# Four edits in a two-layer trunk: other delays, a later constant load, a new planner cost, and six batches whose first product waits for ScalarE

## The chip, the cores and the metric

The kernel runs on one NeuronCore of a Trainium2 chip; the other cores are idle. TensorE (PE in the rows, its weight loads PEld) multiplies, VectorE (DVE) and ScalarE (ACT) do the elementwise work, GpSimd (POOL) almost nothing, and SyncE's queue (SP) issues nearly all transfers. The metric is device time in microseconds (us) of one execution.

## The reference, cut to what matters

Sequence 512, width 1024, float32. Layer 0 has a gated short convolution and a gated linear recurrence (HGRN2) side by side; layer 1 has stick-breaking attention with 16 heads of width 64. Each layer ends with a squared-ReLU MLP of width 4096, and the six modulation vectors of a layer come from one product with `c`.

```python
for layer in range(2):
    mod = silu(c) @ ada_w[layer] + ada_b[layer]
    shift1, scale1, gate1, shift2, scale2, gate2 = split(mod, 6)
    h = rms_norm(x, norm_mix[layer]) * (1 + scale1) + shift1
    y = mixer_conv_hgrn(h, ...) if layer == 0 else mixer_stick_breaking(h, ...)
    x = x + gate1 * y
    h = rms_norm(x, norm_mlp[layer]) * (1 + scale2) + shift2
    x = x + gate2 * (square(relu(h @ w1[layer])) @ w2[layer])
```

## The kernel before, in words

Activations lie transposed: eight tiles of 128 features by 512 positions. Every float32 product is made of three products of a high and a low part (`mm3`, lines 278 to 283: high weight by high input, high by low, low by high). A weight tile of 128x1024 comes by one transfer of 512 KB into one of four buffers of the tag `raw` (line 259); ScalarE casts the high part (`whi`, line 271) and VectorE subtracts for the low part (`wlo`, line 272). Each of `whi` and `wlo` has four buffers too, so a cast waits until TensorE has done the last product with the buffer's old weights.

**The start** (`start`, lines 512 to 664). The eight `x` tiles, sixteen `ada` tiles and eight weight tiles `ws` come on SyncE's queue in a written order (line 40), then the first tile of `wv` and a small constant tile (lines 561, 562). All engines but GpSimd run in an order that a planner makes. For each k of 0 to 7, ScalarE casts the weights (line 667) and makes the high half of `h` (line 640), and TensorE adds 24 products of 512 columns into eight banks (lines 651 and 657). Right after it `late_constants` (lines 409 to 414) loads 480 KB of masks and selectors through ScalarE's own queue into one of the `raw` buffers, and ScalarE copies them out.

**The mixer of layer 0** (lines 677 to 957). TensorE's order is written out by hand: a stream of projections yields every three products of 512 columns (0.64 us in the order's own clock), and a heap of due times puts the stages of the recurrence between them. `hgrn_pair` (lines 765 to 885) runs twice, for heads 0 and 1 and for heads 2 and 3: between two stages it yields the delay `STEPS[pair][stage]` (line 46), then issues 8 to 32 small products of the tiles `Kt` and `Qt` (or `Q`) into a bank `lv` (lines 786, 809, 822, 800, 861, 865), which VectorE and ScalarE fold into `A`. VectorE brings `Kt` and `Qt` up to the next stage (lines 839, 840). `background` puts dots of `ada` tiles (line 419) on VectorE between.

**The MLPs** (`mlp`, lines 1146 to 1206). 32 hidden tiles come in four batches of eight, each followed by up to eight outputs (`second`, `products`, `done`), whose 24 products have 512 columns. In a batch, hidden tiles are made in pairs (`pair`, lines 1081 to 1130) by seven products of half size, each of 12 matmuls of 256 columns, into banks `a`, `b`, `c`; ScalarE copies a finished bank aside (`kept`, line 1102). The first batch begins in `mlp_head`; of the others, b = 1, 2, 3 in each layer, the first pair begins as soon as the output of the batch before is multiplied. The last product of a pair is put off (`last`): that of the fourth pair comes after 21 matmuls of the first output. Weights of the first pair are cast while the last outputs are multiplied (lines 1188 to 1196). Only TensorE's order is fixed here; the order on ScalarE and VectorE is made by the scheduler.

**The attention** (lines 1260 to 1679). All engines follow the order of one planner, `Graph.run`, that puts each operation where it could start first by estimated durations (`dve_us(n)` is 0.068 + 0.00104 n us, line 217). A unit (a pair of heads by one to two query blocks) has products (lines 1514, 1515), sigmoids on ScalarE (line 1522), a scan and a product on VectorE (lines 1526, 1528), transposes on TensorE (line 1542) with a copy back (line 1544), and products with `v` (line 1563).

Of the kernel before, what the change touches and what calls it, by code (L numbers as in the profile page):

```python
# [20 lines left out]
ALU = mybir.AluOpType  # L21
# [21 lines left out]

PARTS = ((0, 1), (2, 3, 4), (5, 6, 7))

STEPS = ((4.5, 7.0, 3.4, 2.5, 2.2, 2.5, 3.5, 2.5, 2.2, 2.5), (3.4, 8.5, 2.8, 2.5, 2.5, 2.8, 2.5, 2.5, 2.5, 2.5))
SHIFT1, SCALE1, GATE1, SHIFT2, SCALE2, GATE2 = range(6)


# [171 lines left out]
def trunk(tc, x_d, c_d, rep_d, small_d, const_d, ada_d, ws_d, win_d, wv_d, woab_d, w1_d, w2_d, wqk_d, wvc_d, woc_d, out_d):  # L221
# [186 lines left out]

    def late_constants():
        ctmp = wp.tile([P, 1024], F32, name="ctmp", tag="raw", bufs=4)  # L410
        act.dma_start(ctmp[:, :C_END - C_SEL], const_d[:, C_SEL:C_END])
        act.copy(sel, ctmp[:, 0:512])
        act.copy(sel4, cons[0:4, C_SEL4:C_SEL4 + P])
        act.copy(lvl, ctmp[:, 512:512 + 7 * 64])
# [255 lines left out]

    wv0 = start()
    start_s.close()
    late_constants()

# [49 lines left out]
    for j in range(2):  # L726
        begun = do_hf(sacc[4 + j], F2, j, 2 + j)
    for j in range(2):
        act.copy(Q2[:, j], sacc[6 + j])

    vt = [mp.tile([P, T], F32, name=f"vt{t}", tag=f"vt{t}") for t in range(4)]

    def v_g():

        vps = [acc() for _ in range(4)]
        w = wv0
        for c in range(4):
            for kk in range(2):
                k = 2 * c + kk
                for t in range(4):  # L740
                    wc = slice(kk * T, (kk + 1) * T)
                    hh, hl = hT[k][0][:, ks(t)], hT[k][1][:, ks(t)]
                    pe.matmul(vps[t], hh, w[0][:, wc], start=(k == 0), stop=False)
                    pe.matmul(vps[t], hh, w[1][:, wc], start=False, stop=False)
                    pe.matmul(vps[t], hl, w[0][:, wc], start=False, stop=(k == NT - 1))
                    yield 0.64
                if kk == 0 and c < 3:

                    with tc.issue_after((begun if c else evicted).ins):
                        wn = load_w(wv_d[c + 1])  # L750
            w = wn
        for t in range(4):
            act.copy(vt[t], vps[t])
# [324 lines left out]
        split(r1[:, b], *w[3])  # L1078
        yield w

    def pair(i, hp, th, hid, before, steps_):


        for w in steps_:
            pass
        wa, wb, wc, wd = w
        a, b, c = [acc(256) for _ in range(3)]
        cm = [hp.tile([P, T], F32, name="cm", tag="cm", bufs=3) for _ in range(2)]
        out = [hid_new(hp, 2 * i + j) for j in range(2)]
        hid += out  # L1090
        b11 = [(hT[k], H[0]) for k in range(4)]
        b21 = [(hT[k], H[0]) for k in range(4, 8)]
        b22 = [(hT[k], H[1]) for k in range(4, 8)]
        t1, t2, t3, t4 = [[(t_, slice(256 * k, 256 * k + 256)) for k in range(4)] for t_ in th]

        def prod(ps, w, at, bs, first):
            for k, (h, sl) in enumerate(bs):
                mm3(ps, w, slice(at + k * P, at + (k + 1) * P), h, sl, first and k == 0, k == 3, skip_group_check=True)

        def kept(ps):  # L1100
            t_ = hp.tile([P, 256], F32, name="kept", tag="kept", bufs=5)
            act.copy(t_, ps)
            return t_

        def relu2(j, sl, ps=None):
            c_ = cm[j][:, sl]
            act.activation(c_, c_ if ps is None else ps, AF.Relu)
            act.activation(c_, c_, AF.Square)
            split(cm[j], *out[j], sl)

        prod(a, wa, 0, b11, True)
        p1 = kept(a)
        prod(c, wb, 0, t1, True)
        p5 = kept(c)
        before()
        prod(a, wb, T, t2, False)
        u2 = kept(a)
        prod(b, wa, T, b21, True)
        dve.tensor_tensor(cm[0][:, H[0]], b, p1, op=ALU.add)
        prod(c, wc, 0, b22, False)  # L1120
        dve.tensor_tensor(cm[0][:, H[1]], c, u2, op=ALU.add)
        relu2(0, FULL)
        prod(a, wc, T, t3, False)
        dve.tensor_tensor(cm[1][:, H[1]], a, p5, op=ALU.add)
        relu2(1, H[1])

        def last():
            prod(a, wd, 0, t4, False)
            relu2(1, H[0], a)
        return last  # L1130
# [15 lines left out]
    def mlp(l, last, hp, head, th, more=()):  # L1146

        nrm = Norm(1, 0, (7,)) if not last else None
        ahead = None
        for b in range(4):  # L1150
            hid, rest = list(head) if b == 0 else [], lambda: None
            if b == 0:
                for n, j in enumerate((4, 5)):
                    whole_tile(more[n] if more else load_w(w1_d[l, j]), j, hp, hid)
            for i in range(len(hid) // 2, 4):
                rest = pair(4 * b + i, hp, th, hid, rest, ahead or pair_w(l, 4 * b + i, hp))
                ahead = None
            n = 8 if b < 3 else 7 if last else 5
            second = lambda o: (acc(), load_w(w2_d[l, b // 2, o, b % 2], None, AT256 if o == n - 1 else AT512))

            def products(p, k0, k1):
                for k in range(k0, k1):
                    mm3(p[0], p[1], ks(k), hid[k], FULL, k == 0, k == 7)

            def done(o):
                added = x_add(o, ps_[o][0], FULL, l, GATE2)
                if b == 3:
                    if last:
                        sync.dma_start(out_d[o], x[o])
                    else:  # L1170
                        nrm.add(o, FULL)
                if o + 2 < n:
                    ps_[o + 2] = second(o + 2)
                if o < len(PIECES[b]):

                    with tc.issue_after(added.ins):
                        background(PIECES[b][o])

            ps_ = {0: second(0)}
            products(ps_[0], 0, 7)  # L1180
            rest()
            ps_[1] = second(1)
            products(ps_[1], 0, 7)
            for o in range(2):
                products(ps_[o], 7, 8)
                done(o)
            for o in range(2, n):
                if o == n - 2 and b < 3:

                    ahead = pair_w(l, 4 * b + 4, hp)  # L1190
                    next(ahead)
                    next(ahead)
                products(ps_[o], 0, 8)
                done(o)
                if o == n - 2 and b < 3:
                    ahead = [next(ahead)]
        if not last:
            log_exp_tables()
        ps, banks, ws = {}, {}, []
        for o in range(n, 8):  # L1200
            for hf in range(2):
                banks[bank[0] % 8] = o, hf
                ps[o, hf] = acc(256)

            ws.append(load_w(w2_d[l, 1, o, 1], None if o == n else (hp, f"t{o - 6}h", f"t{o - 6}l"), AT256))
        return nrm, ps, banks, hid, ws
# [298 lines left out]
    def unit_z(p, i):  # L1505

        spans, nn, nw = spans_of(i)
        z, om, be = [zts.new() for _ in range(2)], oms[i].new(), bes[i].new()
        K_, Q_, y, ny = KK[p], QQ[p], rq[p][2], rq[p][3]

        def logits(j):
            for b, off, _, n in spans:
                zz, kk = z[j].t[:, off:off + max(256, n)], K_[j].t[:, :max(256, n)]
                pe.matmul(zz, Q_[j].t[:, ks(b)], kk, start=(off == 0), stop=False, skip_group_check=True)
                pe.matmul(zz, Q_[j].t[:, ks(4 + b)], kk, start=False, stop=True, skip_group_check=True)
        for j in range(2):
            on_pe(sum(2 * max(256, n) * 0.00042 for _, _, _, n in spans), lambda j=j: logits(j), (K_[j], Q_[j]), (z[j], om, be), 0)
        for out, sc in ((om, ny), (be, y)):
            for j in range(2):
                for b, off, to, n in spans:  # L1520
                    c, o0 = 2 * b + j, j * nw + to
                    sig.append(on_act(n, lambda out=out, sc=sc, j=j, off=off, n=n, c=c, o0=o0: act.activation(
                        out.t[:, o0:o0 + n], z[j].t[:, off:off + n], AF.Sigmoid, scale=sc.t[:, c:c + 1]), (z[j], sc), (out,), 2, psum=True, column=True))

        s_ = lambda: om.t[:, ::-1]
        on_dve(2 * nw, lambda: dve.tensor_tensor_scan(s_(), s_(), pats[i][:, ::-1], 0.0, op0=ALU.mult, op1=ALU.max), (om,), (om,), 2)  # L1526
        w_ = lambda: be.t[:, :2 * nw - 1]
        on_dve(2 * nw, lambda: dve.tensor_tensor(w_(), w_(), om.t[:, 1:2 * nw], op=ALU.mult), (om, be), (be,), 2)
        return om, be
# [279 lines left out]
```

## Time and profile before

| | |
|---|---|
| time, median of 3 runs | 1232.36 us (1231.9 to 1233.48) |
| profiled execution | 1233.2 us, of which the span of the trace is 1231.4 us |
| PE | 1207.2 us busy (98%), 7657 matmuls |
| PEld, DVE, ACT | 1066.3, 890.1, 610.4 us busy (87%, 72%, 50%) |
| granted TensorE clock, mean | 0.994 of full speed |
| transfers | 163.50 MB, mean 133 GB/s |

The span is the time from the first to the last instruction; 1.8 us of the profiled execution lie around it. A matmul counts as busy from its start to its modelled end, and matmuls overlap, so "busy" says little about TensorE's rate: that is read from the distance of two starts, or from the number of matmuls in a stretch.

### The profile page before, as it was taken

To read this page: it belongs to the slowest core of one execution; us is meant where nothing else is said; L and a number is where in the kernel's file an instruction comes from. 1 tells how busy PE (TensorE), PEld (TensorE's weight loads), DVE (VectorE), ACT (ScalarE), POOL (GpSimd) and SP (SyncE) were. 2 spreads that over 40 slices of the span, in tenths; PEclk is the share of its full clock that TensorE was granted. 3 is DMA by queue.
4 is the path that set the end of the run, shared out by engine and by line. 5 is a ranking of instruction groups with operands and counts; after the bars stand their busy time and mean duration, and the time that the engine had idled before them with its cause. 6 is when DMAs were issued, how large, how long until landed. Compare 5 with 4: busy or idle time off the path is not lost.

```text
span 1231.4 us, 19181 instructions
## 1 busy us (share of the span) xinstructions
PE 1207.2 (98%) x7657; PEld 1066.3 (87%) x7657; DVE 890.1 (72%) x1433; ACT 610.4 (50%) x1101; POOL 13.1 (1%) x24
## 2 busy tenths in 40 slices
PE   7999999999999999999999999999999999999998
PEld 6788887899889899898998878787998898998997
DVE  8898778969687685886866783678695676566652
ACT  4333223437338166264547764677474273472650
POOL 0000000000000000000110000000000000000000
PEclk9999999999999999999989999999999999999999
DMA  8766554621554633734531312232114234133231
GB/s 301 257 221 204 188 179 156 227 89 59 178 209 137 213 130 120 253 106 151 192 90 64 104 47 78 83 103 87 52 36 140 82 105 135 62 127 103 69 121 52
DMA packets 46330, 163.50 MB, mean 133 GB/s; under 512 B 5264, under 2 KB 5784, under 8 KB 46240
## 3 DMA queue, kind: packets, MB, share of 16 engines
q1 hardware_dynamic: 46096, 161.78, 39.5%
q8 instruction: 60, 0.98, 0.3%
q10 hardware_dynamic: 144, 0.49, 0.1%
q14 instruction: 30, 0.25, 0.1%
HBM read 155.96 MB, written 2.10 MB: 128 GB/s over the span
## 4 chain that ended last, share of the span: by engine, by line
PE 74%; DVE 15%; DMA 5%; ACT 4%; issue 2%; SPq 0%; DVEq 0%; ACTq 0%
PE b L281 18%; PE b L283 18%; PE b L282 18%; PE acc L281 3%; PE acc L282 3%; PE acc L283 3%; DVE om L1526 2%; DMA wraw<-in_ada 2%; DVE wlo L272 2%; PE b L1563 1%; PE b L1542 1%; PE b L1598 1%; DMA raw<-in_ws 1%; PE b L1470 1%; PE b L1600 1%
## 5 line engine op out<-in xcount | busy, mean ns | idle before, releaser
L271 ACT CAST whi<-wraw 128x1024 fp32r<-128x1024 f32 x123 | 127.5, 1048 | 229.2 <-PE b L282 79.5
L281 PE MATMUL b<-hidh,whi 128*128 128x512 f32 (+1 forms) x544 | 205.3, 377 | 0.0
L282 PE MATMUL b<-hidl,whi 128*128 128x512 f32 (+1 forms) x544 | 205.1, 377 | 0.0
L283 PE MATMUL b<-hidh,wlo 128*128 128x512 f32 (+1 forms) x544 | 205.0, 377 | 0.0
L281 PE MATMUL b<-hh,whi 128*128 128x256 f32 (+1 forms) x632 | 195.7, 310 | 0.0
L282 PE MATMUL b<-hl,whi 128*128 128x256 f32 (+1 forms) x632 | 192.4, 304 | 0.7 <-DVE hl L1426 0.7
L283 PE MATMUL b<-hh,wlo 128*128 128x256 f32 (+1 forms) x632 | 192.3, 304 | 0.0
L272 DVE TENSOR_TENSOR wlo<-wraw,whi 128x1024 fp32r<-128x1024 f32 x123 | 149.5, 1220 | 43.7 <-ACT whi L271 41.6
L505 DVE SCALAR_TENSOR_TENSOR x<-b,modc,x 128x512 f32<-128x512 f32 (+1 forms) x100 | 67.8, 683 | 95.2 <-PE b L283 95.1
L282 PEld LDWEIGHTS b<-hl,whi 128*128 128x128 f32 x632 | 121.1, 192 | 5.6 <-DVE hl L1426 1.1
L281 PEld LDWEIGHTS b<-hh,whi 128*128 128x128 f32 x632 | 120.0, 190 | 6.1 <-issue 1.7
L283 PEld LDWEIGHTS b<-hh,wlo 128*128 128x128 f32 x632 | 120.0, 190 | 5.3
L283 PEld LDWEIGHTS b<-hidh,wlo 128*128 128x128 f32 x544 | 102.1, 188 | 19.3
L281 PEld LDWEIGHTS b<-hidh,whi 128*128 128x128 f32 x544 | 102.1, 188 | 18.8
L282 PEld LDWEIGHTS b<-hidl,whi 128*128 128x128 f32 x544 | 102.3, 188 | 18.6
L419 DVE CUSTOM_DVE_ANT_0 wraw<-wraw,cb 128x1024 f32<-128x1024 f32 x80 | 96.3, 1218 | 19.5 <-DMA wraw<-in_ada 19.4
L271 ACT CAST whi<-tt 128x1024 fp32r<-128x1024 f32 x52 | 53.3, 1050 | 47.3 <-PE b L282 32.1
L272 DVE TENSOR_TENSOR wlo<-tt,whi 128x1024 fp32r<-128x1024 f32 x52 | 63.3, 1218 | 16.0 <-ACT whi L271 15.1
L291 DVE TENSOR_TENSOR hidl<-cm,hidh 128x256 fp32r<-128x256 f32 (+1 forms) x90 | 45.3, 510 | 40.4 <-ACT hidh L290 39.1
L1376 DVE TENSOR_TENSOR wlo<-raw,whi 128x1024 fp32r<-128x1024 f32 x36 | 43.7, 1222 | 18.7 <-ACT whi L1375 18.3
L281 PE MATMUL acc<-hh,whi 128*128 128x512 f32 x128 | 52.2, 408 | 0.0
L283 PE MATMUL acc<-hh,wlo 128*128 128x512 f32 x128 | 49.9, 390 | 0.0
(375 smaller groups left out, 2633.1 us busy)
## 6 DMA issues: line engine op xcount, KB each, us to landing
wraw<-in_w SPq DMA_DIRECT2D x122, 512.0 KB, 3.4
wraw<-in_ada SPq DMA_DIRECT2D x80, 512.0 KB, 4.1
eraw<-in_ada SPq DMA_DIRECT2D x16, 512.0 KB, 3.7
wraw<-in_win SPq DMA_DIRECT2D x16, 512.0 KB, 3.9
raw<-in_wqk SPq DMA_DIRECT2D x16, 512.0 KB, 5.1
raw<-in_ws SPq DMA_DIRECT2D x8, 512.0 KB, 7.3
wraw<-in_woab SPq DMA_DIRECT2D x8, 512.0 KB, 4.2
raw<-in_wvc SPq DMA_DIRECT2D x8, 512.0 KB, 4.8
```

Of the source, the lines that this page charges most:

```text
L271: act.copy(hi, raw)
L272: dve.tensor_tensor(lo, raw, hi.bitcast(F32), op=ALU.subtract)
L281: pe.matmul(ps, whi, h[0][:, hs], start=start, stop=False, **kw)
L282: pe.matmul(ps, whi, h[1][:, hs], start=False, stop=False, **kw)
L283: pe.matmul(ps, wlo, h[0][:, hs], start=False, stop=stop, **kw)
L291: dve.tensor_tensor(lo[:, sl], t_[:, sl], hi[:, sl].bitcast(F32), op=ALU.subtract)
L419: dve.tensor_tensor_reduce(out=raw, in0=raw, in1=cb, scale=1.0, scalar=0.0, op0=ALU.mult, op1=ALU.add, accum_out=modr[:, col:col + 1])
L505: return dve.scalar_tensor_tensor(x[o][:, sl], ps, mcol(l, v, o), x[o][:, sl], op0=ALU.mult, op1=ALU.add)
L1376: on_dve(1024, lambda: dve.tensor_tensor(lo.t, raw.t, hi.t.bitcast(F32), op=ALU.subtract), (raw, hi), (lo,), 1)
L1470: pe.matmul(col.t[:, 8 * s + 2 * b:8 * s + 2 * b + 2], sq[s].t[:, ks(b)], hs2, start=True, stop=True)
L1526: on_dve(2 * nw, lambda: dve.tensor_tensor_scan(s_(), s_(), pats[i][:, ::-1], 0.0, op0=ALU.mult, op1=ALU.max), (om,), (om,), 2)
L1542: pe.transpose(tp.t[:, o_:o_ + P], be.t[:, w0:w0 + P], ident)
```

## The change

Four edits. The delays `STEPS` between the stages of the recurrence are others. `late_constants` is called inside the product with `wv` instead of right after the start; its transfer goes on SyncE's queue, and its copies stand on ScalarE behind the copy `Q2`. At the first pair of the batches b = 1, 2, 3 of both layers ScalarE copies two columns of the last output's bank into the bank of the first product, before that product's matmuls are issued. And in the attention's planner the scan is given the estimate of a tile twice as wide.

```diff
-STEPS = ((4.5, 7.0, 3.4, 2.5, 2.2, 2.5, 3.5, 2.5, 2.2, 2.5), (3.4, 8.5, 2.8, 2.5, 2.5, 2.8, 2.5, 2.5, 2.5, 2.5))
+STEPS = ((4.5, 6.5, 3.6, 3.7, 2.4, 2.5, 2.5, 2.2, 2.2, 2.2), (1.5, 7.0, 3.4, 3.5, 3.0, 2.8, 2.2, 2.2, 2.2, 2.2))
...
     def late_constants():
         ctmp = wp.tile([P, 1024], F32, name="ctmp", tag="raw", bufs=4)
-        act.dma_start(ctmp[:, :C_END - C_SEL], const_d[:, C_SEL:C_END])
+        sync.dma_start(ctmp[:, :C_END - C_SEL], const_d[:, C_SEL:C_END])
...
     start_s.close()
-    late_constants()
...
-        act.copy(Q2[:, j], sacc[6 + j])
+        copied = act.copy(Q2[:, j], sacc[6 + j])
...
                     with tc.issue_after((begun if c else evicted).ins):
                         wn = load_w(wv_d[c + 1])
+                    if c == 0:
+                        with tc.issue_after(copied.ins):
+                            late_constants()
...
-    def pair(i, hp, th, hid, before, steps_):
+    def pair(i, hp, th, hid, before, steps_, rested):
...
+        if rested is not None and i % 4 == 0:
+            act.copy(a[:, 0:2], rested[:, 0:2])
         prod(a, wa, 0, b11, True)
...
-                rest = pair(4 * b + i, hp, th, hid, rest, ahead or pair_w(l, 4 * b + i, hp))
+                rest = pair(4 * b + i, hp, th, hid, rest, ahead or pair_w(l, 4 * b + i, hp), ps_[7][0] if b else None)
...
-        on_dve(2 * nw, lambda: dve.tensor_tensor_scan(s_(), s_(), pats[i][:, ::-1], 0.0, op0=ALU.mult, op1=ALU.max), (om,), (om,), 2)
+        on_dve(4 * nw, lambda: dve.tensor_tensor_scan(s_(), s_(), pats[i][:, ::-1], 0.0, op0=ALU.mult, op1=ALU.max), (om,), (om,), 2)
```

## Rows read from the trace of the kernel before

**Rows 1.** The page: busy time of the engines, and the chain of waits by engine.
```profile
PE 1207.2 (98%) x7657; PEld 1066.3 (87%) x7657; DVE 890.1 (72%) x1433; ACT 610.4 (50%) x1101; POOL 13.1 (1%) x24
...
PE 74%; DVE 15%; DMA 5%; ACT 4%; issue 2%; SPq 0%; DVEq 0%; ACTq 0%
```

**Rows 2.** Windows of 20 us inside batches of the MLPs, all matmuls of 256 columns: length, then busy time and number of instructions of PE, PEld, DVE, ACT, POOL, granted clock, DMA share, GB/s.
```profile
376.00:396.00 20.00, 20.00 (x179) 20.00 (x178) 15.94 (x25) 16.41 (x33) 0.00 (x0) 1.00 0.35 112
453.00:473.00 20.00, 20.00 (x173) 20.00 (x172) 16.23 (x26) 17.00 (x35) 0.00 (x0) 1.00 0.34 106
989.00:1009.00 20.00, 20.00 (x172) 20.00 (x172) 15.80 (x26) 16.70 (x35) 0.00 (x0) 1.00 0.33 107
```

**Rows 3.** The timeline of PE at two stalls between matmuls of 256 columns: start, length, operation. From 307.24 to 313.48 are the first and the last of 54 matmuls without a stall, from 372.83 to 378.95 the first and the last of 55.
```profile
306.90 0.38 PE L283 MATMUL b<-t0h,wlo 128*128 128x256 f32 x1 [0.66 <-DVE wlo L272]
...
307.24 0.28 PE L282 MATMUL b<-t0l,whi 128*128 128x256 f32 x1
...
313.48 0.28 PE L281 MATMUL b<-t2h,whi 128*128 128x256 f32 x1
...
371.58 0.28 PE L283 MATMUL b<-t3h,wdl 128*128 128x256 f32 x1
371.91 0.38 PE L281 MATMUL b<-t1h,whi 128*128 128x256 f32 x1
372.13 0.28 PE L282 MATMUL b<-t1l,whi 128*128 128x256 f32 x1
...
372.83 0.28 PE L282 MATMUL b<-t1l,whi 128*128 128x256 f32 x1
...
378.95 0.28 PE L282 MATMUL b<-t0l,whi 128*128 128x256 f32 x1
```

**Rows 4.** The timeline of ACT: its smallest operation, the copy that ended the stall of 371.91, a batch's begin at 441.66, a cast and a copy inside that batch, and the begin of the last batch.
```profile
63.09 0.20 ACT L585 ACTIVATE lbe<-lbe 128x12 f32<-128x12 f32 x1
...
371.51 0.35 ACT L1102 COPY kept<-b 128x256 f32<-128x256 f32 x1
...
441.68 1.05 ACT L271 CAST whi<-wraw 128x1024 fp32r<-128x1024 f32 x1 [2.56 <-PE b L282]
...
446.03 1.05 ACT L271 CAST whi<-tt 128x1024 fp32r<-128x1024 f32 x1 [0.97 <-PE b L282]
446.98 0.37 ACT L1102 COPY kept<-b 128x256 f32<-128x256 f32 x1
...
1144.46 1.05 ACT L271 CAST whi<-wraw 128x1024 fp32r<-128x1024 f32 x1 [4.50 <-PE b L282]
```

**Rows 5.** The timeline of PE where the batch of 441.66 begins: the last two matmuls of the output before, and the first of the batch.
```profile
441.20 0.40 PE L282 MATMUL b<-hidl,whi 128*128 128x512 f32 x1
441.43 0.39 PE L283 MATMUL b<-hidh,wlo 128*128 128x512 f32 x1
441.66 0.28 PE L281 MATMUL b<-hh,whi 128*128 128x256 f32 x1
```

**Rows 6.** The end of the start: the timelines of ACT, with its queue's transfer, and of PE, then windows as in rows 2.
```profile
46.00 0.38 ACTq L411 DMA_DIRECT2D ctmp<-in_const  x1
52.98 1.04 ACT L667 CAST whi<-raw 128x1024 fp32r<-128x1024 f32 x1 [6.88 <-DMA raw<-in_ws]
53.93 0.72 ACT L640 ACTIVATE hh<-tt,modc 128x512 fp32r<-128x512 f32 x1
...
52.04 0.61 PE L651 MATMUL misc<-hl,whi 128*128 128x512 f32 x2
54.70 0.50 PE L651 MATMUL acc<-hh,whi 128*128 128x512 f32 x1 [2.04 <-ACT hh L640]
...
48.00:52.00 4.00, 4.00 (x19) 3.34 (x18) 3.46 (x8) 0.00 (x0) 0.00 (x0) 1.00 0.86 313
...
56.00:60.00 4.00, 4.00 (x12) 3.14 (x11) 3.89 (x8) 2.45 (x5) 0.00 (x0) 0.57 0.42 131
```

**Rows 7.** Windows as in rows 2 around two other stalls of PE, and the timeline's row of the second stall.
```profile
622.00:626.00 4.00, 2.02 (x19) 1.93 (x18) 3.17 (x8) 3.86 (x12) 0.00 (x0) 1.00 0.00 0
626.00:630.00 4.00, 4.00 (x22) 4.00 (x21) 0.76 (x3) 0.66 (x2) 0.00 (x0) 0.51 0.00 0
...
863.00:867.00 4.00, 4.00 (x29) 3.08 (x28) 0.99 (x2) 0.59 (x1) 0.00 (x0) 1.00 0.37 131
...
861.59 0.63 PE L1542 MATMUL b<-cons,be 128*128 128x128 f32 x4 [1.54 <-DVE be L1528]
```

**Rows 8.** The mixer: who waited for whom on PE from 60 to 200 us (us in total, times, longest), then the timelines of DVE and PE at two stages of the first pair of heads.
```profile
PE lv L809 <- DVE Kt L840: 2.3, 3, 1.1
...
87.00 0.71 DVE L840 TENSOR_TENSOR Kt<-Kt,T 128x512 f32<-128x512 f32 x1
...
87.93 0.33 PE L809 MATMUL lv<-Qt,Kt 128*128 128x64 f32 x2
...
93.72 0.41 PE L809 MATMUL lv<-Qt,Kt 128*128 128x64 f32 x2 [1.09 <-DVE Kt L840]
```

**Rows 9.** The attention: the group of the widest scans (count, busy us, mean ns, idle before), and who waited for whom from 600 to 925 us.
```profile
L1526 DVE TENSOR_TENSOR_SCAN om<-om,pat 128x1026 f32<-128x1026 f32 x8 | 18.3, 2287 | 1.4 <-ACT om L1522 1.4
...
PE b L1542 <- DVE be L1528: 3.6, 5, 1.5
...
PEld b L1542 <- DVE be L1528: 2.3, 4, 1.2
```

## The prediction, made before the change was run

> **What bounds the kernel now.** I read the page first. TensorE is busy for 98% of the span and owns 74% of the chain of waits [rows 1]. A busy PE says little about its rate, since its matmuls overlap, so I next counted matmuls in windows of the MLPs. [...] By starts in the timeline it is (378.95 - 372.83) / 54 = 113.3 ns after the stall at 371.91, and (313.48 - 307.24) / 53 = 117.7 ns after the one at 306.90 [rows 3]: 4.4 ns apart. Neither stretch waits for anything inside. A stall of TensorE can thus change the spacing of what follows, and need not. Third, the list of waits on PE gives the places where it stands still: the end of the start [rows 6], three stages of the recurrence [rows 8], and the attention [rows 9].
>
> **The sum is made against the profiled execution, 1233.2 us** (a span of 1231.4 and 1.8 around it); the median of the runs is 0.8 lower, which comes off at the end.
>
> **The constant load.** Its transfer is issued at 46.00 on ScalarE's queue. From then to 52.98 ScalarE stands 6.88 us for the last weight tile, whose cast stands before the `hh` that TensorE needs; TensorE's two products from 52.04 on are 0.23 us apart, as those of [rows 5], so it is out of work at 52.5 and resumes at 54.70, 2.2 us later [rows 6]. Without the 480 KB (0.49 MB) beside it, at the 313 GB/s of the window 48 to 52 [rows 6], the weights land 0.49 / 0.313 = 1.6 us sooner. [...] I take 1.6 + 1.6 = -3.2; bounds 0 (the tile was late by its own queue) and -3.8 (all of the stall and of the clock). What the load gets instead: it stands on SyncE's queue behind a `wv` tile, so the other `wv` tiles and the `ada` tiles come behind it, and it holds one of four buffers until ScalarE has copied it behind `Q2`. The three copies have 1088 columns, about 1.1 us plus two starts, against 1.05 us for 1024 [rows 4]; queued behind them on ScalarE are the copies of `Qt` and the casts of the next weights, which the stream wants some microseconds later. I price that at nothing; without that cover it is 1.4 us.
>
> **The delays.** One step of the stream is three matmuls, 0.69 us. Adding up the old and new delays in the order's own clock, the first pair of heads changes between its stages 2 and 3 only: six steps instead of four (the two come off between its stages 5 and 6). That is where PE idles 1.09 us at 93.72 for `Kt` [rows 8]: 1.4 us of stream cover it. In the second pair the first stage comes after 3 steps instead of 6, the next after 11 instead of 14, and the three after that after 6, 6 and 5 instead of 5, 4 and 4. The three waits for `Kt` are 2.3 us in all [rows 8]; I take all of it, -2.3. The other bound is 0: VectorE's `Kt` of the stage before is done at 87.00 + 0.71 = 87.71, only 0.22 us before its products start at 87.93 [rows 8]. If TensorE arrives 3.2 us sooner and VectorE does not, the waits grow again and take up to those 3.2 us back. VectorE starts its own run there on results of TensorE and ScalarE, so I expect it to move along.
>
> **The scan's estimate.** The planner's 0.068 + 0.00104 x 1026 = 1.14 us was for a scan that takes 2.29 us; with the edit it is 2.20 [rows 9]. So 24 scans were planned about 1 us too short each, transposes were put too early, and PE waits for `be` 3.6 us, its weight loads 2.3 us [rows 9]. At best 5.9 us go. But the whole order of the attention is made anew by a greedy plan, and nothing excludes a loss of the same size. I take -1.0.
>
> **The six begins.** First the price. TensorE restarts when ScalarE has copied two columns, which waits for the last matmul of the output (441.43) [rows 5]. A reader on ScalarE starts 0.48 us after the start of the matmul that it waits for (cast at 441.68, matmul at 441.20) [rows 4, 5], so the copy could start at 441.91. A copy of two columns isn't in the trace: it lies between nothing and the 0.37 us of one with 256 columns, nearest to the 0.20 us of one with 12 [rows 4], which I take. From a copy's end (371.51 + 0.35) to the matmul at 371.91 it is 0.05 us, and the matmul after a stall is 0.22 us behind instead of 0.12 [rows 3, 4]. So 442.16 - 441.66 + 0.10 = 0.60 us a stall, 3.6 us for six. But what stands before the copy on ScalarE? At 441.68 a cast of the next pair's weights starts, released by the last product but one, 0.23 us before the copy could start; the last batch has the same at 1144.46. Inside the batch the trace shows this very race: the cast of 446.03 goes ahead and the copy of a finished bank waits for it until 446.98 [rows 4]. If so here, the copy starts at 441.68 + 0.95 = 442.63, TensorE at 442.88, and a stall costs 1.22 + 0.10 = 1.32 us, six 7.9 us. I take this one. A stall of 1.2 us is short of the one that left the clock alone [rows 7].
>
> Then the gain. The first pair has 84 matmuls of 256 columns, all four have 336, of which 12 come after 21 wide ones: 324 x 4.4 ns = 1.43 us where the spacing changes. Five batches are slow throughout (two of them stand in [rows 2]); the first of layer 0 is fast from 371.91 on, so only 9 products, 108 matmuls, gain: 0.48, and its own stall (0.33 - 0.12 + 0.10 = 0.31 [rows 3]) may go, since TensorE comes later. Sum: 5 x 1.43 + 0.48 + 0.3 = 7.9. I expect the change of spacing in most batches, because the stall at 371.91 was made by a copy on ScalarE before a product's first matmul, as here; the one at 306.90 was for a weight's low part. So the six begins come to 0: a gain that its own price eats. Bounds -4.3 (copy ahead of the cast) and +8.5.
>
> **Sum:** -3.2 - 2.3 - 1.0 + 0.0 = -6.5: 1226.7, and 1225.9 beside the median. I say 1226.
>
> **Rivals.**
> - *The copy is ahead of the cast* (its place in the program is earlier; against it the order at 446.03): -4.3 more, 1221.6.
> - *The stalls leave the spacing as it is* (as at 306.90). Its place is the six begins, and it decides from four slow batches of five on. Price 7.9, and the batch of 371.91 loses its chance stall: 216 x 4.4 ns = 0.95, less 0.3. Then +8.5 - 6.5 = +2.0: 1234.4, slower than before. [...]
> - *TensorE only comes sooner to VectorE*: the 3.2 us of the start are lost again in the stages of the recurrence [rows 8]: -3.3, 1229.1.
>
> **Chances.** Forecast 0.40, copy ahead 0.22, spacing unchanged 0.20, start given back 0.18. A measurement here can tell about 0.2% (2.5 us) from no change. Faster by more than that: nearly all of the first two, half of the last, a little of the third: 0.71. Within: half of the third, a third of the last and a few hundredths: 0.17. Slower: 0.12, the third with a bad plan of the attention. Range 1218 to 1235.5, which reaches to both outer rivals with part of the plan's bounds; the forecast's own is 1222 to 1230.
>
> **What would show it.** Start: no transfer of `ctmp` at 46, PE's stall near 54 under 1 us, clock 1.00 from 56 to 60. Delays: no rows of L809 waiting for `Kt`. Scan: fewer waits of L1542 for `be`. Begins: six stalls of PE on ScalarE of about 1.2 us, the copy behind a cast of `whi`, and 176 to 179 matmuls in 20 us afterwards; 172 or 173 would make the spacing wrong, stalls of 0.5 us the order on ScalarE. The forecast is wrong if the time is above 1230 or under 1222.

## The result, and the profile after

The changed kernel takes 1236.84 us (median of six executions, 1234.15 to 1240.73), the kernel before 1232.51 beside it (six, 1229.42 to 1233.48): 1.0042 of its time, 95% interval 1.0026 to 1.0059. That is slower by 0.4%, and above the range.

The profiled execution of the changed kernel took 1240.73 us, the longest of its six; its span is 1238.9, 7.5 us above that of before. Starts of the same matmuls in both timelines tell where (us):

| first matmul of | before | after | gained or lost since the row above |
|---|---|---|---|
| the product with `wv` | 67.32 | 63.05 | -4.27 |
| the mixer's last projection | 224.76 | 222.34 | +1.85 |
| the MLP of layer 0, product of `t0h` | 305.84 | 303.66 | +0.24 |
| the tail after its last batch | 591.96 | 605.30 | +15.52 |
| the MLP of layer 1, product of `t0h` | 925.00 | 932.92 | -5.42 |
| the last matmul | 1227.90 | 1235.42 | -0.40 |

One stretch loses nearly everything: the MLP of layer 0 with its three begins. That of layer 1, with three begins of the same code, is even. First the page after, with busy time and the chain by engine [rows 1]; in the first, TensorE is busy for 1.6 us less in a span that is 7.5 us longer, so it stands still for some 9 us more.

```profile
PE 1205.6 (97%) x7657; PEld 1064.4 (86%) x7657; DVE 890.0 (72%) x1433; ACT 610.7 (49%) x1107; POOL 12.8 (1%) x24
...
PE 79%; DVE 12%; DMA 6%; ACT 2%; issue 1%; SPq 0%; DVEq 0%; ACTq 0%
```

Then the new copy's own view: its durations, what it waited for, and who waited for it (us, times).

```profile
L1115 ACT COPY b<-b x6: 145/145/145, 361.4 to 1153.1; 128x2 f32<-128x2 f32 x6
its engine sat idle before it (us, times) until:
  DVE x L505: 9.6, 3
who waited for it (us, times):
  PEld b L281: 18.6, 6
  PE b L281: 16.0, 6
```

The copy itself is short, 0.145 us. But three of the six waited for line 505 on VectorE, the addition of the output to `x`, and TensorE waited 16.0 us for the six. The timelines of one begin in each layer follow; PE, DVE and ACT of layer 0 first.

```profile
356.09 0.39 PE L283 MATMUL b<-hidh,wlo 128*128 128x512 f32 x1
361.56 0.58 PE L281 MATMUL b<-hh,whi 128*128 128x256 f32 x1 [5.08 <-ACT b L1115]
...
356.61 1.22 DVE L272 TENSOR_TENSOR wlo<-tt,whi 128x1024 fp32r<-128x1024 f32 x1
357.74 0.69 DVE L1071 TENSOR_TENSOR tt<-wraw 128x512 f32<-128x512 f32 x1
...
359.97 0.69 DVE L1071 TENSOR_TENSOR tt<-wraw 128x512 f32<-128x512 f32 x1 [0.34 <-DMA wraw<-in_w]
360.58 0.75 DVE L505 SCALAR_TENSOR_TENSOR x<-b,modc,x 128x512 f32<-128x512 f32 x1
...
361.36 0.14 ACT L1115 COPY b<-b 128x2 f32<-128x2 f32 x1 [3.98 <-DVE x L505]
```

The last matmul of the output starts at 356.09. VectorE then makes a low part and four sums of the next pairs' weights, one of them after a wait for its transfer, and only then the addition, 360.58 to 361.33. The copy starts 0.03 us later, TensorE after it. Now layer 1:

```profile
985.60 0.39 PE L283 MATMUL b<-hidh,wlo 128*128 128x512 f32 x1
987.01 0.38 PE L281 MATMUL b<-hh,whi 128*128 128x256 f32 x1 [1.02 <-ACT b L1115]
...
986.03 0.75 DVE L505 SCALAR_TENSOR_TENSOR x<-b,modc,x 128x512 f32<-128x512 f32 x1 [2.15 <-PE b L283]
...
985.80 1.04 ACT L271 CAST whi<-wraw 128x1024 fp32r<-128x1024 f32 x1 [4.50 <-PE b L282]
986.81 0.14 ACT L1115 COPY b<-b 128x2 f32<-128x2 f32 x1
```

Here VectorE is idle and adds at once (986.03 to 986.78), while ScalarE makes the cast that stands before the copy, and the begin goes nearly as forecast. Even so the addition ends last: the copy starts 0.03 us behind its end, as in layer 0, and 1.01 us behind the cast's start, where 0.95 is the usual distance [rows 4]. That is some 0.05 us of the stall. From start to start (before: 0.23 us) the six stalls are 5.47, 5.03 and 3.57 us in layer 0 and 1.41 three times in layer 1. Windows as in rows 2, 6 and 7: the end of the start, the stretch behind a stall of the mixer, behind the three stalls of layer 0, behind one of layer 1, and inside three batches.

```profile
52.00:56.00 4.00, 4.00 (x20) 3.30 (x18) 3.90 (x9) 2.10 (x3) 0.00 (x0) 1.00 0.42 144
56.00:60.00 4.00, 4.00 (x19) 3.31 (x18) 3.93 (x9) 1.76 (x4) 0.00 (x0) 1.00 0.46 135
152.00:156.00 4.00, 4.00 (x20) 3.52 (x19) 3.52 (x7) 0.00 (x0) 0.00 (x0) 0.61 0.55 170
361.00:365.00 4.00, 3.44 (x18) 3.44 (x19) 3.86 (x6) 0.52 (x2) 0.00 (x0) 0.57 0.23 70
449.00:453.00 4.00, 3.27 (x15) 3.27 (x16) 2.84 (x4) 0.46 (x2) 0.00 (x0) 0.60 0.31 89
538.00:542.00 4.00, 3.99 (x21) 3.99 (x22) 2.12 (x3) 0.37 (x1) 0.00 (x0) 0.57 0.43 134
987.00:991.00 4.00, 3.99 (x35) 4.00 (x36) 1.10 (x1) 0.74 (x2) 0.00 (x0) 1.00 0.41 129
376.00:396.00 20.00, 20.00 (x179) 20.00 (x178) 16.28 (x25) 17.07 (x36) 0.00 (x0) 1.00 0.35 119
453.00:473.00 20.00, 20.00 (x171) 20.00 (x170) 13.49 (x20) 14.31 (x29) 0.00 (x0) 0.99 0.19 62
989.00:1009.00 20.00, 20.00 (x178) 20.00 (x178) 14.20 (x21) 14.88 (x31) 0.00 (x0) 1.00 0.24 79
```

Each long stall is followed by a granted clock of about 0.6 over 4 us (0.61, 0.57, 0.60 and 0.57 in the rows of 152, 361, 449 and 538), most of it at 0.50, as in each half microsecond from 361.5 to 364.5; the stall of 1.41 us is not (1.00 from 987 to 991). The spacing in the batches is 178 or 179 matmuls per 20 us in five of six (172 for those of before), and 171 in the one of 453.

The sum for the begins in this execution: stalls beyond 0.23 us, 5.24 + 4.80 + 3.34 + 3 x 1.18 = 16.9; the 324 matmuls of 256 columns of each, from the first start to that of the next matmul behind them, 37.54 + 5 x 38.16 = 228.3 us before and 38.23 + 39.80 + 38.47 + 3 x 36.84 = 227.0 after. So +15.6 where the prediction has 0.0. The three stretches at the lower clock are in it: 38.23 - 36.84, 39.80 - 38.27 (its own spacing at full clock) and 38.47 - 36.84 make about 4.5. The table has the same from outside: +15.52 in layer 0 and -0.40 in layer 1.

In a second profiled execution (h1_after_again, below) the stalls of layer 0 are 4.06, 3.84 and 3.43 us, those of layer 1 again 1.41.

### The profile page after: what moved, and what is told of

Read it like the earlier page. It is cut to its first block, busy times and chain, and to the rows that moved or that the text cites. A ratio compares the mean times of both kernels' runs of the same rounds, so it can differ in the third digit from the quotient of the medians.

```text
span 1238.9 us, 19182 instructions
## 1 busy us (share of the span) xinstructions
PE 1205.6 (97%) x7657; PEld 1064.4 (86%) x7657; DVE 890.0 (72%) x1433; ACT 610.7 (49%) x1107; POOL 12.8 (1%) x24
## 4 chain that ended last, share of the span: by engine, by line
PE 79%; DVE 12%; DMA 6%; ACT 2%; issue 1%; SPq 0%; DVEq 0%; ACTq 0%
PE b L281 18%; PE b L282 17%; PE b L283 17%; DMA wraw<-in_w 3%; PE acc L281 3%; PE acc L282 3%; PE acc L283 3%; DMA wraw<-in_ada 2%; DVE wlo L272 2%; PE b L1568 2%; DVE wraw L419 2%; PE b L1547 1%; PE acc L651 1%; PE b L1603 1%; PE b L1605 1%; PE b L1604 1%
## 5 line engine op out<-in xcount | busy, mean ns | idle before, releaser
L505 DVE SCALAR_TENSOR_TENSOR x<-b,modc,x 128x512 f32<-128x512 f32 (+1 forms) x100 | 67.8, 683 | 91.8 <-PE b L283 91.3
L1531 DVE TENSOR_TENSOR_SCAN om<-om,pat 128x772 f32<-128x772 f32 (+2 forms) x24 | 46.3, 1934 | 7.2 <-ACT om L1527 7.2
```

What stands on the lines that cost most here:

```text
L505: return dve.scalar_tensor_tensor(x[o][:, sl], ps, mcol(l, v, o), x[o][:, sl], op0=ALU.mult, op1=ALU.add)
L1531: on_dve(4 * nw, lambda: dve.tensor_tensor_scan(s_(), s_(), pats[i][:, ::-1], 0.0, op0=ALU.mult, op1=ALU.max), (om,), (om,), 2)
```

## The experiments

Times are medians with the lowest and highest execution, ratios to the kernel before on the same chip with a 95% interval. Where a run has some of the four edits alone, it has just their lines of the diff above. A profiled execution can lie up to 8 us from the median of its kernel, so traces are read for places and lengths here, and what an edit yields is read from the medians.

**The copy alone, and all but the copy.** One run has the other three edits and `rested` as None, the other the copy alone:

```diff
-                rest = pair(4 * b + i, hp, th, hid, rest, ahead or pair_w(l, 4 * b + i, hp), ps_[7][0] if b else None)
+                rest = pair(4 * b + i, hp, th, hid, rest, ahead or pair_w(l, 4 * b + i, hp), None)
```

> The changed kernel without the copy of two columns (delays, constant load and scan estimate as changed). In the profiled execution of the changed kernel the first three edits had gained 2.3 us by the first batch of layer 0 and another 5.4 us in the attention, and the three begins of layer 0 had lost 15.4 us. Theory (the copy waits for VectorE's add): the begins go back to their old place, about 7.7 us below the kernel before, 1223 to 1226 us. Rival (the other edits cost it, the begins are neutral as I predicted): 1232 us or more.

> The kernel before with the copy of two columns alone. Theory: three stalls of 3.5 to 5.5 us in layer 0, each followed by a stretch of 3.4 us at the lower clock, and three of 1.4 us in layer 1 with 113 ns between matmuls after them: 10 to 16 us above the kernel before, 1242 to 1248 us. Rival (the begins are neutral): within 2 us of the kernel before.

Without the copy 1224.07 us (1221.19 to 1225.62), ratio 0.9915 [0.9899, 0.9931]; with the copy alone 1245.66, 1.0109 [1.009, 1.0127]. The copy alone makes the kernel slower than all four edits do, and its stalls have the pattern of the changed kernel: 4.56, 4.27 and 4.22 us in layer 0, 1.41 three times in layer 1.

```profile
L1112 ACT COPY b<-b x6: 145/145/145, 363.1 to 1157.9; 128x2 f32<-128x2 f32 x6
its engine sat idle before it (us, times) until:
  DVE x L505: 8.6, 3
```

**The copy ahead of VectorE's addition.** The copy is made where the output is finished, in the line before the addition, so that in the program's order it comes first:

```diff
-        a, b, c = [acc(256) for _ in range(3)]
+        a = rested[0] if rested and i % 4 == 0 else acc(256)
+        b, c = [acc(256) for _ in range(2)]
...
                 products(ps_[o], 0, 8)
+                if o == 7 and b < 3:
+                    a_ = acc(256)
+                    held = a_, act.copy(a_[:, 0:2], ps_[7][0][:, 0:2])
                 done(o)
```

> The changed kernel with the copy of two columns issued ahead of VectorE's add of the last output, so that it waits for TensorE alone. Theory: all six stalls are about 1.2 us over the usual distance, as those of layer 1 were (the copy still stands behind a cast), no lower clock after them, most batches at 113 ns: within 2 us of the kernel without the copy, 1222 to 1227 us. Rival (in layer 0 something other than the add holds the copy, such as a full ScalarE): stalls of 3.5 to 5.5 us stay there, 1236 us.

1226.03 us (1219.97 to 1228.65), 0.993 [0.9907, 0.9952]. Stalls 1.40, 1.40, 1.40, 1.36, 1.36, 1.36 us, and all six batches at 113 ns. The 324 matmuls take 36.83 to 36.84 us in the five without a further stall, so no lower clock stands behind those stalls: with one in it a batch at that spacing took 38.23 and 38.47 us in the changed kernel. The same two columns cost 11 us less than in the changed kernel by the medians, 14 by the ratios, only because of what stands before them. The begin that the prediction worked out at 441.66, in the timelines of ACT, PE and DVE:

```profile
441.80 1.04 ACT L271 CAST whi<-wraw 128x1024 fp32r<-128x1024 f32 x1 [2.65 <-PE b L282]
442.75 0.15 ACT L1199 COPY b<-b 128x2 f32<-128x2 f32 x1
...
441.55 0.39 PE L283 MATMUL b<-hidh,wlo 128*128 128x512 f32 x1
442.96 0.38 PE L281 MATMUL b<-hh,whi 128*128 128x256 f32 x1 [1.01 <-ACT b L1199]
443.18 0.29 PE L282 MATMUL b<-hl,whi 128*128 128x256 f32 x1
...
445.12 0.74 DVE L505 SCALAR_TENSOR_TENSOR x<-b,modc,x 128x512 f32<-128x512 f32 x1
```

The copy waits for TensorE and for the cast, nothing else, as the prediction has it; the addition comes over 2 us later, and nobody waits for it.

**The cast out of the copy's way.** The cast of the next pair's weights is held behind the copy (e5), then also behind the first bank that is copied aside (e6), so that it doesn't run beside the product either:

```diff
+        with tc.issue_after(rested[1].ins) if rested and i % 4 == 1 else ExitStack():
+            for w in steps_:
+                pass
```

> As the one before, and the cast of the next pair's weights is put behind the copy on ScalarE. Theory (price of a stall by what stands before the copy): stalls of 0.4 to 0.6 us, and 113 ns in most batches; 0.8 us less for each of six begins, 4 to 5 us below the run before, 1217 to 1222 us. Rival (shorter stalls do not change the spacing, or the later cast delays the next pair's weights): no faster than the kernel without the copy.

> As the kernel with the copy ahead of the add and the cast behind the copy, but the cast stands behind the batch's first kept copy too, so that ScalarE is idle when TensorE restarts after the short stall of 0.62 us. Theory (the cast that runs at the restart kept the spacing at 118 ns): 113 ns after the stalls in most batches, 0.9 us less per batch than without the copy, 1217 to 1221 us. Rival (a stall of this length leaves the spacing alone, whatever ScalarE does): 118 ns, 1225 to 1229 us.

The stalls shrink to 0.62 us in both, but all six batches begin at 118 ns and all but one stay there (38.27 us; in the first batch of e6 a stall of 0.53 us inside it, at 371.52, brings 113): 1227.05 us, 0.9945 [0.9924, 0.9966], and 1227.6, 0.9954 [0.9937, 0.9971]. A shorter stall gained nothing here, since the spacing behind it didn't change.

**The other three edits, each alone.**

> The kernel before with the later constant load alone. In the profiled run of the changed kernel the product with wv began 4.2 us sooner and 2.7 us of it were left at the end of the mixer. My prediction's term: -3.2 us, with 0 as the other end if VectorE's stages give it back. Theory A: -2 to -3.5 us, 1229 to 1232. Theory B (given back in the stages of the recurrence with the old delays): 0 to -1 us.

> The kernel before with the new delays alone. My prediction's term: -2.3 us, all the waits of L809 for Kt gone. Theory A: -1.5 to -2.7 us. Theory B (the changed kernel showed a stall of 2.5 us at stage 3 of the second pair with the lower clock behind it, so the second pair now comes too soon for VectorE): 0 to +2 us, with that stall in the trace.

> The kernel before with the scan's doubled estimate alone. My prediction's term: -1 us; the traces of the changed kernel and of the one without the copy show 5.4 and 6.6 us less between the tail of layer 0 and the second MLP. Theory A (a truer plan puts the transposes where their input is ready): -5 to -7 us, 1226 to 1229, and PE's waits for be at least halved. Theory B (the gain came from the shifted work before it): -1 us or less.

> The kernel before with the scan's estimate and the late constants, and neither the new delays nor the two-column copies. Theory A (the start's gain of the late constants is lost in the mixer's waits for Kt whatever the attention's order is): 1226 to 1229 us, that of the scan's estimate alone. Theory B (it was lost only by the waits of the attention, which the estimate takes away): 1222 to 1225, the time of the version with all but the copies or better.

The late constants alone: 1233.09 us beside 1233.06, 0.9991 [0.9976, 1.0006]. The delays alone: 1235.95, 1.0011 [0.9995, 1.0027]. The estimate of the scan alone: 1227.98, 0.9945 [0.9925, 0.9966], 6.8 us. Estimate and late constants: 1224.25, 0.9912 [0.9891, 0.9933]. The last one points to some gain of the constants once the attention's waits are gone, but the two intervals overlap.

With the late constants alone the product with `wv` starts at 63.7 instead of 67.3, the MLP of layer 0 at 303.4 instead of 305.8, its second batch at 441.1 instead of 441.7, and the last matmul at 1228.2 instead of 1227.9. Windows of that kernel:

```profile
56.00:60.00 4.00, 4.00 (x19) 3.13 (x18) 3.90 (x9) 1.31 (x2) 0.00 (x0) 1.00 0.26 71
...
146.00:150.00 4.00, 4.00 (x14) 3.14 (x13) 3.76 (x6) 0.00 (x0) 0.00 (x0) 0.62 0.41 131
...
630.00:634.00 4.00, 4.00 (x21) 4.00 (x21) 0.84 (x2) 2.02 (x4) 0.00 (x0) 0.53 0.00 0
```

The start's gain is there (19 matmuls from 56 to 60, 12 before). It goes piece by piece: at a stage of the recurrence with a lower clock behind it (0.62, 14 matmuls from 146 to 150), at a stall of 1.44 us inside the first batch with 118 ns behind it, which in before was 0.33 us long and brought 113 ns, and at a longer stretch of lower clock after 623 (10.2 us; 6.8 before).

The estimate's gain is in the waits on PE: from 600 to 925 the rows for `be` [rows 9] are gone from the list, and this is all of it:

```profile
PE b L1470 <- ACT nsq L1455: 2.0, 1, 2.0
PE b L282 <- DVE hl L1426: 0.7, 2, 0.5
PE b L281 <- ACT kept L1102: 0.5, 1, 0.5
```

**Does the length of the stall decide the spacing?** So far stalls of 1.36 us and more at a begin and at full clock brought 113 ns and those of 0.62 didn't. Into the last kernel with 0.62 us (e6) come one (g1) or two (g2; g4 is the same kernel profiled again) copies of 256 columns ahead of the small one, with no cast beside:

```diff
                     a_ = acc(256)
+                    act.copy(a_, ps_[7][0][:, 0:256])
                     held = [a_, act.copy(a_[:, 0:2], ps_[7][0][:, 0:2])]
```

> The version with the six stalls of 0.62 us (next pair's cast out of the way), with one more copy of 256 columns ahead of the two-column copy on ScalarE, so that each stall is some 0.25 to 0.40 us longer: 0.87 to 1.02 us from start to start, by the 0.37 us of a copy of 256 columns in its own trace. Theory A (the length of the stall decides the spacing, somewhere between 0.62 us, after which none of six batches was fast, and 1.36 us, after which all were): says nothing sure of this length; it narrows the gap: all six fast or all six slow. Theory B (the cast of weights that runs beside TensorE's first matmul decides, not the length): all six slow, 118 ns.

> The same with two more copies of 256 columns ahead of the two-column copy, so that each stall is 1.1 to 1.4 us without any cast beside it. Theory A (length decides): 113 ns in all six batches, 36.84 us for their first 324 matmuls if the stall comes near 1.36 us. Theory B (the cast decides): 118 ns in all six, 38.2 us. By either no lower clock after the stalls.

> The version with six stalls of 1.40 us and no cast beside them, a second time and on its own: its profiled execution took 1224 us, eight timed ones between 1230 and 1235. Theory A (a stall of that length always brings the faster spacing, and the other executions lost their time elsewhere): 113 ns in all six batches, 36.84 us for 324 matmuls, whatever the time. Theory B (the spacing after a stall differs from execution to execution): if this execution takes 1230 us or more, several batches at 118 ns. If it takes about 1224 us again, the two are not told apart.

Stalls of 1.01 us: all six at 113 ns, 1220.89 us (1217.91 to 1224.77), 0.9894 [0.9867, 0.9921]. Stalls of 1.40 us: all six at 113 ns in the profiled execution, which took 1224.17 us; the median of nine is 1232.21, the other eight 1230.1 to 1234.72, 0.9982 [0.9961, 1.0004]. The second profiled execution of the same kernel (g4, 1232.77 us) has the same stalls of 1.40 us and all six batches at 118 ns. A window of 20 us inside the fifth begin's batch, of the first:

```profile
1062.00:1082.00 20.00, 20.00 (x179) 20.00 (x178) 16.20 (x26) 17.30 (x35) 0.00 (x0) 1.00 0.33 107
```

and of the second:

```profile
1062.00:1082.00 20.00, 20.00 (x173) 20.00 (x172) 15.59 (x23) 15.26 (x30) 0.00 (x0) 1.00 0.24 80
```

The six batches take 222.1 us in the first (37.83 for the one with a stall of 0.99 us inside it, 36.85 for the others) and 229.6 in the second: 7.5 of the 8.6 us by which the two executions differ. So the kernel alone doesn't fix the spacing. Four of the kernels above, unchanged, in a second profiled execution:

> The changed kernel in a second profiled execution. By either theory the six stalls are there again with the same lengths, to some 0.1 us: three of 3.5 to 5.5 us in layer 0, each with a stretch at the lower clock behind it, and three of 1.41 us in layer 1. Theory A (the kernel decides the spacing that follows): layer 1 at 113 ns in all three batches, as in its first profiled execution. Theory B (the execution decides): layer 1 at 118 ns, all three alike, is as likely; the time is then some 4 us longer for the same stalls.

> The version whose two-column copy is traced ahead of VectorE's addition, in a second profiled execution; stalls of 1.36 to 1.40 us. Theory A (the kernel decides): 113 ns in all six batches, about 1226 us. Theory B (the execution decides): all six at 113 or all six at 118 ns; with 118 the time is about 8 us above what it would be with 113.

> The version with six stalls of 1.01 us and no cast beside them, in a second profiled execution (all six at 113 ns in the first). Theory A: 113 ns again, 1218 to 1225 us. Theory B: all six at 113 or all six at 118 ns.

> The version with six stalls of 0.62 us and no cast beside them, in a second profiled execution (all six at 118 ns in the first). Theory A, in the form that a stall under 1 us never brings the faster spacing: 118 ns again. Theory B (the execution decides): all six at 113 is as likely, and the time is then near 1219 us.

They took 1235.61, 1228.83, 1221.0 and 1220.53 us. The changed kernel: layer 1 at 113 ns in all three, layer 0 at 118, 118, 113. Copy first: 118, 113, 118, then 113 three times. Stalls of 1.01 us: all six at 113. Stalls of 0.62 us: all six now begin at 113, where the first execution had 118 at all six begins; the first batch is at 113 only until a stall of 1.61 us inside it, at 373.17, and at 118 behind that. The same window as above in the first execution with the stalls of 0.62 us (e6),

```profile
1062.00:1082.00 20.00, 20.00 (x172) 20.00 (x171) 15.45 (x26) 16.23 (x33) 0.00 (x0) 1.00 0.34 106
```

and in the second:

```profile
1062.00:1082.00 20.00, 20.00 (x179) 20.00 (x178) 16.51 (x27) 17.32 (x37) 0.00 (x0) 1.00 0.34 107
```

Over all profiled executions, begins without a stall: 0 of 36 at 113 ns. After 0.62 us 6 of 18, after 1.01 us 12 of 12, after 1.36 to 1.41 us 25 of 33, after 3.4 to 5.5 us 4 of 9.

## Why the prediction was wrong, step by step

**The step that failed** is the first of the price of the begins: "TensorE restarts when ScalarE has copied two columns, which waits for the last matmul of the output (441.43)". It waits for VectorE's addition of that output, which reads the same bank and stands before it in the program. In layer 1 the addition ran beside the cast and cost some 0.05 us; in layer 0 it came so late that the stalls were 3.3 to 5.2 us longer than no stall at all, and the lower clock followed (0.57 to 0.60 over 4 us). The run with the copy ahead of the addition shows it: with that order alone exchanged, all six stalls were 1.36 to 1.40 us, 1.36 where they had been 1.41. The prediction named the copy's producer and the engine that runs it, but not the bank's other reader. The row was there: in the kernel before, the output whose last matmul starts at 441.43 is added here,

```profile
440.89 0.68 DVE L1069 TENSOR_TENSOR tt<-wraw 128x512 f32<-128x512 f32 x1
...
444.50 0.74 DVE L505 SCALAR_TENSOR_TENSOR x<-b,modc,x 128x512 f32<-128x512 f32 x1
```

behind six sums of weights, where nobody waited for it. A copy at 445.24 would have meant, by estimate, a stall of about 4.0 us from start to start and a lower clock behind it, as behind those of 3.57 to 5.47 us in the changed kernel's profiled execution (0.57 to 0.60); three of those are 11 us of standing still.

In the timelines shown the two reads of the bank don't overlap, in either order: the copy at 361.36 behind the addition that ends at 361.33, and with the copy first (442.75, 0.15 us long) the addition at 445.12, though there 2 us lie between them. That the program's order makes the copy wait, rather than the bank itself, is argued from the exchange and from the row that names the addition as what released the copy (3.98 <-DVE x L505); it wasn't measured apart.

**The price where the addition is in time**: 1.32 us forecast; measured 1.41 - 0.23 = 1.18, and 0.10 for the slower next matmul (0.22 instead of 0.12), 1.28. The copy was put at 0.20 us and takes 0.145. The cast did go ahead of it, in layer 1 and in all six begins of the run with the copy first, so the rival with the copy ahead falls.

**The gain behind a stall**: 1.43 us a batch forecast; 38.16 - 36.84 + 0.10 = 1.42 measured. But the forecast took it as following from every stall; over all profiled executions it followed 25 of 33 of that length. Price and gain nearly cancel, as written: copy first (1226.03) against no copy (1224.07) shows no gain from the six copies.

**The rival with unchanged spacing** was wrong as a rule and right in single executions: the second one with the stalls of 1.40 us (g4) is what it describes. At full clock these streams have 113 or 118 ns in the profiled executions, and one kernel has both in two of them (36.85 and 38.27 us for the same 324 matmuls, g2 and g4).

**The constant load**, -3.2: right at its place in the pair of traces compared (the product with `wv` 3.6 us earlier with this edit alone, PE without a gap at 54, clock 1.00 from 56 to 60 in the changed kernel). But that place moves from execution to execution: the product starts at 64.7 to 67.3 in the four profiled executions without the edit (mean 66.2) and at 62.6 to 65.0 in the fourteen with it (mean 63.9), so 2.3 us is the better figure, and of it 1.2 are left at the MLP of layer 0 (means 305.7 and 304.6; most of the fourteen have the other edits too). The second 1.6 us of the forecast are for the clock: no run shows them apart from the earlier weights; the windows from 56 to 60 show 12 matmuls at 0.57 in the kernel before [rows 6] and 19 at 1.00 with the edit, 7 x 0.23 = 1.6 us. The yield alone was 0.0 by the medians and -1.1 by the ratio, interval -3.0 to +0.7: the rival "start given back" held for it alone, though only in part by the stages of the recurrence that it named.

**The delays**, -2.3: gave nothing alone, +0.1% [-0.05, 0.27]. The wait at 93.72 went; another took its place. Who waited for whom on PE from 60 to 200 us in the kernel with the delays alone, then in the changed kernel:

```profile
PE lv L809 <- DVE Kt L840: 2.5, 1, 2.5
...
PE lv L811 <- DVE Kt L842: 2.7, 2, 2.4
```

and the longest of the latter's waits in the timeline of PE:

```profile
151.49 0.74 PE L811 MATMUL lv<-Q,Kt 128*128 128x64 f32 x5 [2.36 <-DVE Kt L842]
```

That is 2.5 and 2.7 us against the 2.3 of [rows 8], in fewer and longer waits. The longest one is in the second pair of heads in both kernels; in the changed kernel it has a lower clock behind it, 0.61 from 152 to 156. The prediction had counted the stream that covers the first pair's wait (1.4 us) and nothing for the second pair, whose first two stages it brought six steps forward; that this brought TensorE there ahead of VectorE is argued from the counts.

**The scan's estimate**, -1.0: the sign was right and the size off: -6.8 us alone (interval -9.2 to -4.2), about the 5.9 us of waits for `be` that bounded it. The term was undersized because 4.9 of the 5.9 us were set against a possible loss by the new plan; the waits went nearly whole. In the profiled execution of that edit the granted clock was also 1.00 from 622 to 630, where before it was 0.51 from 626 to 630 [rows 7]. That isn't all of the gain: the 6.8 us at the lower clock (0.50) before cost about 3.4 us by estimate, and the way from the tail of layer 0 to the MLP of layer 1 took 333.0 us before and 323.2 with the estimate. In the executions of the copy alone and of the delays alone it took 329.5 and 329.8 us.

Together, as the changed kernel's own trace has it: -2.2 until the first MLP, +15.5 in that MLP, -5.4 in the attention, -0.4 in the second MLP. Without the copies 1224.07 us were measured, near the 1226 forecast, but by luck: of the 10.5 us below the kernel before, the estimate alone gave 6.8, where the forecast had put 5.5 of its 6.5 on the start and the delays. Estimate and late constants gave 10.9 without the delays.

## What to carry to other kernels

Before an instruction is made to read a tile that others read, list the other readers and where their engines stand: here a new reader behind a late one in the program's order took over all of its lateness (it started 0.03 us behind its end). A consumer that nobody waits for shows no wait in the profile, however late it runs (here the addition at 444.50, its last matmul at 441.43); look for the distance between producer and consumer in the engine's timeline, not for a wait. And a repair that works by disturbing another engine's rhythm needs several profiled executions of the same kernel: one trace showed all of the gain here and the next none. Fastest here were the version with stalls of 1.01 us (1220.89 us) and that without the copies (1224.07); both beat the kernel before and the changed one, and their intervals overlap.

## What was not expected of the hardware

The spacing of matmuls of 256 columns at full clock has two levels in these traces, 113.3 and 117.8 ns, and a stall can set either. Between stalls it holds for a whole batch (38.16 us for the 324 matmuls in five batches of the kernel before), within one execution it is mostly the same after all stalls of one kind, and between two executions of one kernel it differed in all six. Not once in 36 begins without a stall was the shorter one there. What chooses is open: not the length alone (1.40 us: six of six, then none of six), nor the cast beside it (none in g1, where all six were short). In the changed kernel's first execution the stalls of 2.4 to 5.5 us at 151, 361, 449 and 538 were each followed by a granted clock of about 0.6 over the next 4 us (0.61, 0.57, 0.60, 0.57); in the second the one of 3.43 us was not (its 324 matmuls took 36.84 us). Behind stalls of 1.41 us and shorter at the begins no lower clock shows where the length of a batch or the clock stands above: 36.83 to 36.85 us at 113 ns, 38.27 at 118, and 1.00 from 987 to 991.
